# One matmul of 512 columns in place of two of 256 in the MLP's input product

## The chip, the cores and the metric

The kernel runs on one NeuronCore of a Trainium2 chip (trn2). The metric is the device time of one execution in microseconds, the median of three runs: 2261.78 us before the change (2261.63 to 2261.96).

## The reference

Two layers of a hybrid encoder over 256 tokens of width 2048, in float32. Each layer normalises x, projects it, runs two kinds of attention, projects back and adds; then comes the MLP that the change touches, with a hidden width of 8192:

```python
h = rmsnorm(x, mlp_norm[l])
u = jax.nn.relu(jnp.einsum('bsd,df->bsf', h, w_mlp_in[l]))
x = x + jnp.einsum('bsf,fd->bsd', u * u, w_mlp_out[l])
```

## The kernel before

**Precision.** TensorE multiplies in a reduced float32 format (fp32r). To keep the accuracy of float32, every operand is split into a high half (the value rounded to fp32r) and a low half (what is left), and a product is the sum of three: high by high, low by high, high by low.

**The weight stream.** All weights arrive as 384 slabs of 1 MB, [128, 2048], through SyncE's DMA queue into three `raw` buffers (`next_slab`, L112). Each slab is split in two pieces of 1024 columns: ScalarE writes the high half `whi` (L130), VectorE subtracts and writes the low half `wlo` (L131). There are four buffers of each, enough for two slabs.

**Two kinds of product.** `block_product` (L140) makes 256 tokens by 512 outputs: the activations are the stationary operand and 512 columns of a slab the moving one, so each of its matmuls moves 512 columns (L153 to L155), 24 of them per slab. `stationary_product` (L173) is turned round: 128 columns of the slab are stationary, and the moving operand is one half of the normalised, transposed activations, `h_t[k]`, 256 tokens wide. One slab holds all 16 blocks of 128 rows (k) for 128 outputs, and each k takes three matmuls: weight high by activation high (L180), weight high by activation low (L181), weight low by activation high (L182). `h_t[k]` is one tile [128, 2, 256], its two halves side by side.

**Who uses which.** The input and output projections and the MLP's second product go through `block_product`. The neighbourhood heads' q and k (32 slabs) and the MLP's first product (64 slabs in each of two layers, 128 in all) go through `stationary_product`.

**The MLP.** In four chunks (L519) of 16 slabs each, the first product leaves 128 hidden units by 256 tokens in a PSUM tile `accu`. ScalarE makes relu of it (`rl`, L524), VectorE multiplies the two (`u2`, L526), and `split` (L136, L137) makes the halves `u2T`, the stationary operand of the second product, which follows for the chunk's 16 slabs. PSUM accumulators (`acc`, `accu`) rotate through four buffers.

**What sets the order.** Weight loads keep the program's order. Everything else is ordered at build time by a scheduler that simulates the engines; each engine then executes its own list in that order. The scheduler mixes the end of one stage with the start of the next: at the start of an MLP the transposes of x (L221) stand between matmuls of the first slabs.

Of the kernel before, what the change touches and what calls it, by code (L numbers as in the profile page):

```python
# [18 lines left out]
P = 128  # L19
# [16 lines left out]
NB = 512  # L36
NEG = -1.0e30
RUN = 5 * RPB_C + GRID_W
# Where a query of column 0 and an even row finds its last neighbour in a head's reversed table.
RPB_FIRST = RPB_HEAD - 1 - (10 * RPB_C + GRID_W - 1 + WIN_C - 1)  # L40
N_CHUNK = 4
F_PER_CHUNK = D_FF // P // N_CHUNK
SLABS = 48 + 16 + 64 + 64
# Column blocks of 512 of the input projection: q, k, v of the differential heads 0-3, then 4-7.
DIFF_BLOCKS = [0, 2, 4, 1, 3, 5]
NA_Q, NA_K, NA_V = 3 * HALF, 4 * HALF, 5 * HALF

# [1 line left out]
def body(ctx, tc, x, x_t, w, gains_in, gains_o, final_g, lam_in, rpb, ident_in, rope_in, mask_in, out):  # L49
# [5 lines left out]
    small = ctx.enter_context(tc.tile_pool(name="small", bufs=4))  # L55
    ps = ctx.enter_context(tc.tile_pool(name="ps", bufs=2, space=PSUM))

# [1 line left out]
    gin = const.tile([P, 2 * DEPTH, NK], F32, name="gin")  # L59
    nc.scalar.dma_start(gin, gains_in)  # L60
    ident = const.tile([P, P], F32, name="ident")
# [3 lines left out]
    xs = [const.tile([P, D], F32, name=f"x{t}") for t in range(NT)]  # L65

    def stream(dst, src):
        """A load on the queue of the weights, in the order of the program."""
        tc.keep_in_program_order(nc.sync.dma_start(dst, src))

    lam_sb = [None]

    def load_table(l):
        """The relative position biases of a layer, from where each query reads its windows."""
        table = act.tile([P, HEADS, RUN + 1], F32, name="table", tag="table", bufs=1)
        for rr in range(P // GRID_W):
            src = bass.AP(tensor=rpb.tensor,
                          offset=rpb.offset + l * HEADS * RPB_HEAD + RPB_FIRST + rr * RPB_C,
                          ap=[[1, GRID_W], [RPB_HEAD, HEADS], [1, RUN]])
            stream(table[rr * GRID_W:(rr + 1) * GRID_W, :, :RUN], src)  # L80
        return table
# [23 lines left out]
    ones = const.tile([P, P], F32, name="ones")  # L105
    nc.vector.memset(ones, 1.0)

# [1 line left out]
    slab_no = [0]  # L109
    x_rest = [None]  # L110

# [26 lines left out]
                                       op0=ALU.mult, op1=ALU.subtract)  # L138

    def block_product(n_k, operand, before=None, split_tail=0):  # L140
        """[256, 512] = sum over n_k blocks of 128 of operand(k)^T @ the next slabs. The last
        `split_tail` slabs are held together, so that one tile of tokens ends before the other."""
        acc = [ps.tile([P, NB], F32, name="acc", tag="acc", bufs=4) for _ in range(NT)]
        parts = []
        todo = []

        def one(k, t):
            hi, lo = parts[k // 2]
            c0 = (k % 2) * NB
            a = operand(k)  # L150
            wh, wl = hi[:, c0:c0 + NB], lo[:, c0:c0 + NB]
            ah, al = a[:, 0, t * P:(t + 1) * P], a[:, 1, t * P:(t + 1) * P]
            nc.tensor.matmul(acc[t], ah, wh, start=k == 0, stop=False)  # L153
            nc.tensor.matmul(acc[t], al, wh, start=False, stop=False)  # L154
            nc.tensor.matmul(acc[t], ah, wl, start=False, stop=k == n_k - 1)  # L155

        n_s = n_k // 4
        for s in range(n_s):
            if before is not None:
                before(s)  # L160
            parts += next_slab()
            todo += range(4 * s, 4 * s + 4)
            if s < n_s - split_tail:
                for k in todo:
                    for t in range(NT):
                        one(k, t)
                todo = []
        for t in range(NT):
            for k in todo:
                one(k, t)  # L170
        return acc

    def stationary_product(h_t):  # L173
        """[128, 256] = the next slab^T @ normed activations, transposed."""
        parts = next_slab()
        acc = ps.tile([P, S], F32, name="accu", tag="acc", bufs=4)
        for k in range(NK):
            hi, lo = parts[k // 8]
            wh, wl = hi[:, (k % 8) * P:(k % 8 + 1) * P], lo[:, (k % 8) * P:(k % 8 + 1) * P]
            nc.tensor.matmul(acc, wh, h_t[k][:, 0], start=k == 0, stop=False)  # L180
            nc.tensor.matmul(acc, wh, h_t[k][:, 1], start=False, stop=False)  # L181
            nc.tensor.matmul(acc, wl, h_t[k][:, 0], start=False, stop=k == NK - 1)  # L182
        return acc

# [1 line left out]
    def rms_scale(ss, n, width):  # L186
        """(ss / width + EPS) ** -0.5 on [128, n]."""
        v = small.tile([P, n], F32, name="v")
        nc.gpsimd.tensor_scalar(v, ss, 1.0 / width, EPS, op0=ALU.mult, op1=ALU.add)
        r = small.tile([P, n], F32, name="r")  # L190
        nc.gpsimd.tensor_tensor(r, v, mhalf[:, :n], op=ALU.pow)
        return r

    class Norm:
        """RMSNorm of x in pieces: the gain goes into the transposed halves, the scale of
        each token comes out of `scale()` and is applied to the products."""

        def __init__(self, gain):
            self.gain = gain
# [12 lines left out]
            self.h_t[k] = h  # L212

        def take(self, n):
            """Columns n*512... of x are final."""
            for t in range(NT):
                self.squares(n, t)
            for k in range(4 * n, 4 * n + 4):
                pt = ps.tile([P, S], F32, name="tp", tag="tp", bufs=2)
                for t in range(NT):  # L220
                    nc.tensor.transpose(pt[:, t * P:(t + 1) * P], xs[t][:, k * P:(k + 1) * P], ident)  # L221
                self.store(k, pt)
# [5 lines left out]
                self._r[t] = rms_scale(tot, 1, D)  # L228
            return self._r[t]

# [1 line left out]
    def to_sbuf_rope(acc, r, which):  # L232
        """Rotary position of q (which 0) or k (which 1), then transposed: [(m d), head, token]."""
        dst = [act.tile([P, 4, S], F32R, name="qkT", tag="A", bufs=12) for _ in range(2)]
        for t in range(NT):
            nat = work.tile([P, NB], F32, name="nat", tag="nat", bufs=3)
# [41 lines left out]
        return hi, lo  # L278

    def along_free(r):  # L280
        """[128, 256]: r of every token, in all partitions."""
        pb = ps.tile([P, S], F32, name="tp", tag="tp", bufs=2)
        for t in range(NT):
            diag = work.tile([P, P], F32, name="diag", tag="o", bufs=4)
            nc.vector.tensor_scalar(diag, ident, r[t], None, op0=ALU.mult)
            nc.tensor.matmul(pb[:, t * P:(t + 1) * P], ones, diag, start=True, stop=True)
        rb = work.tile([P, S], F32, name="rb", tag="rb", bufs=1)
        nc.scalar.activation(rb, pb, AF.Copy)
        return rb

    def transposed_weights(pr):
        """[128 queries, tile, 256 keys] -> [128 keys, tile, 256 queries] in PSUM."""
        pw = ps.tile([P, NT, S], F32, name="tp", tag="tp", bufs=2)
        for t in range(NT):
            for kt in range(NT):
                nc.tensor.transpose(pw[:, kt, t * P:(t + 1) * P], pr[:, t, kt * P:(kt + 1) * P], ident)  # L296
        return pw

    def weights_times_v(pr, v, j):
        """pr [128 q, tile, 256 keys] -> [128 q, tile, 128] in PSUM."""  # L300
        pw = transposed_weights(pr)
        wt = work.tile([P, NT, S], F32, name="wT", tag="wT", bufs=3)
        nc.scalar.activation(wt, pw, AF.Copy)
# [5 lines left out]
        return po  # L309

    def to_mix(po, scale, gain):
        """Scaled rows of po, transposed, with the gain, split."""
        o = work.tile([P, NT, HD], F32, name="o", tag="o", bufs=4)
        for t in range(NT):
            nc.vector.tensor_scalar(o[:, t, :], po[:, t, :], scale[:, t:t + 1], None, op0=ALU.mult)
# [110 lines left out]
            else:  # L426
                nc.vector.scalar_tensor_tensor(sl, acc[t], scale[t], sl, op0=ALU.mult, op1=ALU.add)

# [1 line left out]
    norm = Norm(0)  # L430

    def prologue(s):
        """The transposed x comes in beside the first slabs, x itself and the tables behind them."""
        st = act.tile([P, 4, S], F32, name="xT", tag="A", bufs=12)

        def load(k0, k1):
            stream(st[:, k0:k1], x_t[s, :, k0:k1])
            for k in range(k0, k1):
                norm.store(4 * s + k, st[:, k, :])

        if s == 0:
            load(0, 2)
            x_rest[0] = lambda: load(2, 4)
        else:
            load(0, 4)

    for l in range(DEPTH):
        if l == 0:
            first = [block_product(NK, norm.h_t.__getitem__, before=b) for b in (prologue, load_constants)]
            for t in range(NT):  # L450
                for n in range(4):
                    norm.squares(n, t)
            # lambda, and the sub-norm's gain times 1 - lambda_init
            lq = lam_sb[0].rearrange("p l (a b) d -> p l a b d", b=2)
            prod = work.tile([P, DEPTH, 2, QKD], F32, name="prod", tag="o", bufs=4)
            for i in range(DEPTH):
# [62 lines left out]
        for c in range(N_CHUNK):  # L519
            us = []  # L520
            for f in range(F_PER_CHUNK):
                acc = stationary_product(h_t)
                rl = work.tile([P, S], F32, name="rl", tag="o", bufs=4)
                nc.scalar.activation(rl, acc, AF.Relu)  # L524
                u2 = work.tile([P, S], F32, name="u2", tag="o", bufs=4)
                nc.vector.tensor_mul(u2, acc, rl)  # L526
                if f % 2 == 0:
                    pair = act.tile([P, 2, 2, S], F32R, name="u2T", tag="A", bufs=12)
                split(pair[:, f % 2, 0], pair[:, f % 2, 1], u2, 1.0)
# [13 lines left out]
                        nxt.take(n)  # L543
        norm = nxt

# [1 line left out]
    for t in range(NT):  # L547
        r = norm.scale(t)
        for n in (3, 0, 1, 2):
# [27 lines left out]
def _pack_weights(w_in, w_out, w_mlp_in, w_mlp_out):  # L577
    slabs = np.empty((DEPTH, SLABS, P, 2048), np.float32)

    def moving(a):  # L580
        """[K, N] -> [N / 512, K / 512, 128, 4 * 512]"""
        K, N = a.shape
        a = a.reshape(K // NB, 4, P, N // NB, NB).transpose(3, 0, 2, 1, 4)
        return a.reshape(N // NB, K // NB, P, 2048)

    def stationary(a):
        """[2048, N] -> [N / 128, 128, 16 * 128]"""
        return a.reshape(NK, P, -1, P).transpose(2, 1, 0, 3).reshape(-1, P, 2048)

    for l in range(DEPTH):  # L590
# [54 lines left out]
```

## Time and profile before

| | |
|---|---|
| time, median of 3 | 2261.78 us |
| span of the profiled execution, first to last instruction | 2259.7 us |
| its own time | the span and what lies around it; 2.1 us separate the span from the median |
| TensorE matmul busy | 2244.5 us, 99%, 13904 matmuls |
| TensorE weight load busy | 2019.3 us, 89%, 13904 loads |
| VectorE, ScalarE, GpSimd busy | 57%, 47%, 4% |
| DMA | 183 GB/s mean over the span |
| mean granted TensorE clock | 0.999 of full speed |

How to read it: matmuls are pipelined, so one matmul's duration in the records (284 ns for 256 columns) is longer than the time it takes from the next one. What counts is the pitch: the distance from the start of one matmul to the start of the next. The chain that ended last gives each matmul its pitch, and the timeline gives starts.

### The profile page before, as it was taken

How to read it: one execution, taken by the hardware profiler on the slowest of the kernel's cores; microseconds unless marked ns; L12 is line 12 of the kernel's file. 1: busy time of each engine (PE TensorE's matmuls, PEld its weight loads, DVE VectorE, ACT ScalarE, POOL GpSimd, SP SyncE). 2: the span in 40 equal slices, each digit the busy share in tenths (PEclk: the TensorE clock that was granted, in tenths of full speed). 3: DMA queues.
4: the chain of work that ended last, by engine and by line, in shares of the span. 5: the costliest groups of instructions: out<-in, count | busy, mean ns of one | idle time of the engine just before them, and what ended most of it. 6: DMA issues, size and time to landing. Idle time of an engine off the chain costs nothing.

```text
span 2259.7 us, 33741 instructions
## 1 busy us (share of the span) xinstructions
PE 2244.5 (99%) x13904; PEld 2019.3 (89%) x13904; DVE 1296.5 (57%) x1615; ACT 1063.4 (47%) x1579; POOL 91.9 (4%) x136
## 2 busy tenths in 40 slices
PE   8999999999999999999999999999999999999998
PEld 7889998998998898899888899989989989988986
DVE  6656666655555555555566666665555555555554
ACT  6556454543444444344445564545434434444443
POOL 1111000000000000000010110000000000000000
PEclk9999999999999999999999999999999999999999
DMA  9453445555555545555654434455555555455553
GB/s 326 149 186 135 173 161 186 184 179 196 187 187 186 190 183 189 198 178 185 202 188 162 168 140 170 179 191 180 187 188 186 186 193 192 179 197 189 186 188 131
DMA packets 61306, 414.63 MB, mean 183 GB/s; under 512 B 7008, under 2 KB 9184, under 8 KB 11872
## 3 DMA queue, kind: packets, MB, share of 16 engines
q1 hardware_dynamic: 60720, 411.40, 50.8%
q8 instruction: 109, 1.79, 0.3%
q10 hardware_dynamic: 432, 1.08, 0.2%
q14 instruction: 45, 0.37, 0.0%
HBM read 410.35 MB, written 2.10 MB: 183 GB/s over the span
## 4 chain that ended last, share of the span: by engine, by line
PE 99%; DMA 0%; DVE 0%; ACT 0%; SPq 0%; issue 0%; POOL 0%; ACTq 0%; POOLq 0%
PE acc L155 18%; PE acc L153 18%; PE acc L154 18%; PE accu L180 14%; PE accu L182 14%; PE accu L181 14%; PE tp L307 1%; PE tp L296 1%; PE tp L221 0%; PE sc L343 0%; DMA raw<-in_w 0%; PE tp L257 0%; PE sc L345 0%; PE sc L344 0%; PE tp L412 0%; PE sc L387 0%
## 5 line engine op out<-in xcount | busy, mean ns | idle before, releaser
L131 DVE TENSOR_TENSOR wlo<-raw,whi 128x1024 fp32r<-128x1024 f32 (+1 forms) x770 | 945.7, 1229 | 848.0 <-ACT whi L130 841.4
L130 ACT ACTIVATE whi<-raw 128x1024 fp32r<-128x1024 f32 (+1 forms) x770 | 814.7, 1059 | 1055.5 <-PE acc L154 548.9
L181 PE MATMUL accu<-hT,whi 128*128 128x256 f32 x2560 | 726.0, 284 | 0.0
L182 PE MATMUL accu<-hT,wlo 128*128 128x256 f32 x2560 | 724.6, 283 | 0.0
L180 PE MATMUL accu<-hT,whi 128*128 128x256 f32 x2560 | 724.0, 283 | 0.0
L181 PEld LDWEIGHTS accu<-hT,whi 128*128 128x128 f32 x2560 | 491.5, 192 | 0.5
L180 PEld LDWEIGHTS accu<-hT,whi 128*128 128x128 f32 x2560 | 490.8, 192 | 0.8
L182 PEld LDWEIGHTS accu<-hT,wlo 128*128 128x128 f32 x2560 | 491.4, 192 | 0.0
L154 PE MATMUL acc<-whi,u2T 128*128 128x512 f32 x1024 | 399.2, 390 | 0.0
L153 PE MATMUL acc<-whi,u2T 128*128 128x512 f32 x1024 | 398.7, 389 | 0.0
L155 PE MATMUL acc<-wlo,u2T 128*128 128x512 f32 x1024 | 398.5, 389 | 0.0
L155 PEld LDWEIGHTS acc<-wlo,u2T 128*128 128x128 f32 x1024 | 192.3, 188 | 39.7
L153 PEld LDWEIGHTS acc<-whi,u2T 128*128 128x128 f32 x1024 | 192.3, 188 | 39.6
L154 PEld LDWEIGHTS acc<-whi,u2T 128*128 128x128 f32 x1024 | 192.3, 188 | 39.3
L153 PE MATMUL acc<-whi,hT 128*128 128x512 f32 x512 | 202.7, 396 | 6.0 <-ACT whi L130 6.0
L154 PE MATMUL acc<-whi,hT 128*128 128x512 f32 x512 | 203.0, 397 | 0.0
L155 PE MATMUL acc<-wlo,hT 128*128 128x512 f32 x512 | 199.4, 395 | 0.1
L153 PEld LDWEIGHTS acc<-whi,hT 128*128 128x128 f32 x512 | 96.9, 189 | 26.3 <-ACT whi L130 6.2
L155 PEld LDWEIGHTS acc<-wlo,hT 128*128 128x128 f32 x512 | 96.7, 189 | 20.3 <-DVE wlo L131 0.5
L154 PEld LDWEIGHTS acc<-whi,hT 128*128 128x128 f32 x512 | 96.9, 189 | 19.7
L154 PE MATMUL acc<-whi,mix 128*128 128x512 f32 x256 | 100.7, 393 | 0.0
L153 PE MATMUL acc<-whi,mix 128*128 128x512 f32 x256 | 100.7, 393 | 0.0
(117 smaller groups left out, 1331.9 us busy)
## 6 DMA issues: line engine op xcount, KB each, us to landing
raw<-in_w SPq DMA_DIRECT2D x383, 1024.0 KB, 4.8
x<-in_x SPq DMA_DIRECT2D x2, 1024.0 KB, 9.7
out<-xg SPq DMA_DIRECT2D x8, 256.0 KB, 3.1
table<-in_rpb SPq DMA_DIRECT2D x4, 438.0 KB, 11.5
xT<-in_x_t SPq DMA_DIRECT2D x3, 512.0 KB, 9.5
raw<-in_w SPq DMA_DIRECT2D x4, 256.0 KB, 5.4
gb<-in_final_g ACTq DMA_DIRECT2D x2, 512.0 KB, 5.7
xT<-in_x_t SPq DMA_DIRECT2D x2, 256.0 KB, 3.5
```

Source lines behind the costliest of these rows:

```text
L130: nc.scalar.activation(hi[:, c:c + step], r, AF.Copy)
L131: nc.vector.tensor_sub(lo[:, c:c + step], r, hi[:, c:c + step].bitcast(F32))
L153: nc.tensor.matmul(acc[t], ah, wh, start=k == 0, stop=False)
L154: nc.tensor.matmul(acc[t], al, wh, start=False, stop=False)
L155: nc.tensor.matmul(acc[t], ah, wl, start=False, stop=k == n_k - 1)
L180: nc.tensor.matmul(acc, wh, h_t[k][:, 0], start=k == 0, stop=False)
L181: nc.tensor.matmul(acc, wh, h_t[k][:, 1], start=False, stop=False)
L182: nc.tensor.matmul(acc, wl, h_t[k][:, 0], start=False, stop=k == NK - 1)
L296: nc.tensor.transpose(pw[:, kt, t * P:(t + 1) * P], pr[:, t, kt * P:(kt + 1) * P], ident)
L307: nc.tensor.matmul(po[:, t, :], wt[:, kt, t * P:(t + 1) * P], v[:, kt, j * HD:(j + 1) * HD], start=kt == 0, stop=kt == NT - 1)
```

## The change

`wide_product` takes the place of `stationary_product` in the MLP; the neighbourhood heads keep the old function. For each slab it first issues sixteen matmuls of the weights' high half against both activation halves at once (512 columns, `h_t[k]` flattened, into a PSUM tile `accw` of 512 columns), then sixteen of the weights' low half against the activations' high half (256 columns, added into the first 256 columns of `accw`). The columns 256 to 511 then hold the part low by high, and have to be added: ScalarE copies them to SBUF (`low`), VectorE adds the two parts (`whole`). VectorE makes relu and square in one operation on SBUF data, `max(u, 0) * u`. `low` is a new tile with two buffers, and the scratch space reserved for the DMA descriptors that GpSimd can write is set to 4096 bytes. Comments are gone, which shifts line numbers.

```diff
+    def wide_product(h_t):
+        parts = next_slab()
+        acc = ps.tile([P, NB], F32, name="accw", tag="acc", bufs=4)
+        for k in range(NK):
+            hi = parts[k // 8][0]
+            nc.tensor.matmul(acc, hi[:, (k % 8) * P:(k % 8 + 1) * P], h_t[k].rearrange("p a b -> p (a b)"),
+                             start=k == 0, stop=False)
+        for k in range(NK):
+            lo = parts[k // 8][1]
+            nc.tensor.matmul(acc[:, :S], lo[:, (k % 8) * P:(k % 8 + 1) * P], h_t[k][:, 0],
+                             start=False, stop=k == NK - 1)
+        low = work.tile([P, S], F32, name="low", tag="low", bufs=2)
+        nc.scalar.activation(low, acc[:, S:], AF.Copy)
+        whole = work.tile([P, S], F32, name="whole", tag="o", bufs=4)
+        nc.vector.tensor_add(whole, acc[:, :S], low)
+        return whole
...
             for f in range(F_PER_CHUNK):
-                acc = stationary_product(h_t)
-                rl = work.tile([P, S], F32, name="rl", tag="o", bufs=4)
-                nc.scalar.activation(rl, acc, AF.Relu)
+                u = wide_product(h_t)
                 u2 = work.tile([P, S], F32, name="u2", tag="o", bufs=4)
-                nc.vector.tensor_mul(u2, acc, rl)
+                nc.vector.scalar_tensor_tensor(u2, u, 0.0, u, op0=ALU.max, op1=ALU.mult)
...
-    nc = bacc.Bacc("TRN2", target_bir_lowering=False, num_devices=1)
+    nc = bacc.Bacc("TRN2", target_bir_lowering=False, num_devices=1, dynamic_dma_scratch_size=4096)
```

The next rows are TensorE's list before, in the middle of a chunk of the MLP's first product, where slab `whi_4315`/`wlo_4316` gives way to the next (`hT` numbers are the blocks k, 4026 the last, 3708 the first).

```order
L180 MATMUL accu_4319<-hT_4020,whi_4315 128x256
L181 MATMUL accu_4319<-hT_4020,whi_4315 128x256
L182 MATMUL accu_4319<-hT_4020,wlo_4316 128x256
L180 MATMUL accu_4319<-hT_4026,whi_4315 128x256
L181 MATMUL accu_4319<-hT_4026,whi_4315 128x256
L182 MATMUL accu_4319<-hT_4026,wlo_4316 128x256
L180 MATMUL accu_4385<-hT_3708,whi_4377 128x256
```

The same place now, first where a slab's high half ends and its low half begins.

```order
L192 MATMUL accw_4315<-hT_4014,whi_4311 128x512
L192 MATMUL accw_4315<-hT_4020,whi_4311 128x512
L192 MATMUL accw_4315<-hT_4026,whi_4311 128x512
L196 MATMUL accw_4315<-hT_3708,wlo_4308 128x256
L196 MATMUL accw_4315<-hT_3714,wlo_4308 128x256
L196 MATMUL accw_4315<-hT_3720,wlo_4308 128x256
```

Three matmuls of 256 columns per k became one of 512 and, sixteen matmuls later, one of 256; a slab's low half is first read in the second part of its slab.

VectorE's list before, over one slab of the same stage: the square, the activations' low half, and between them the two pieces of a later slab's low half.

```order
L526 TENSOR_TENSOR u2_4829<-accu_4778,rl_4827 128x256
L131 TENSOR_TENSOR wlo_4967<-raw_4964,whi_4966 128x1024
L137 SCALAR_TENSOR_TENSOR u2T_4765<-u2_4829,u2T_4765 128x256
L131 TENSOR_TENSOR wlo_4971<-raw_4964,whi_4970 128x1024
L526 TENSOR_TENSOR u2_4894<-accu_4843,rl_4892 128x256
```

VectorE's list now, over one slab (`accw_4572`, whose weights came as `raw_4562`; the slabs after it are 4614, 4665 and 4717).

```order
L201 TENSOR_TENSOR whole_4607<-accw_4572,low_4605 128x256
L543 SCALAR_TENSOR_TENSOR u2_4609<-whole_4607 128x256
L137 SCALAR_TENSOR_TENSOR u2T_4611<-u2_4609,u2T_4611 128x256
L131 TENSOR_TENSOR wlo_4720<-raw_4717,whi_4719 128x1024
L131 TENSOR_TENSOR wlo_4724<-raw_4717,whi_4723 128x1024
```

One operation per slab was added, the sum `whole`; the low half made behind it is that of the slab three further on.

At the start of an MLP, TensorE's list before, around the first use of a block (`hT_4008`) from the last 512 columns of x (`x0_79` and `x1_80` are x's two tiles, `tp` the transposes).

```order
L182 MATMUL accu_4123<-hT_3908,wlo_4120 128x256
L180 MATMUL accu_4057<-hT_4008,whi_4053 128x256
L180 MATMUL accu_4123<-hT_3914,whi_4119 128x256
L181 MATMUL accu_4123<-hT_3914,whi_4119 128x256
L182 MATMUL accu_4123<-hT_3914,wlo_4120 128x256
L180 MATMUL accu_4123<-hT_3920,whi_4119 128x256
L221 MATMUL tp_4017<-ident_75,x0_79 128x128
```

And now:

```order
L192 MATMUL accw_4160<-hT_3920,whi_4156 128x512
L192 MATMUL accw_4160<-hT_3926,whi_4156 128x512
L240 MATMUL tp_4017<-ident_75,x0_79 128x128
L240 MATMUL tp_4017<-ident_75,x1_80 128x128
L192 MATMUL accw_4057<-hT_4008,whi_4053 128x512
L192 MATMUL accw_4109<-hT_4008,whi_4105 128x512
L192 MATMUL accw_4160<-hT_4008,whi_4156 128x512
L240 MATMUL tp_4023<-ident_75,x0_79 128x128
```

Before, two slabs had been begun at that point; now three have, and 36 matmuls of 512 columns stand ahead of the first use of `hT_4008`. Outside the MLP's first product TensorE's and SyncE's lists hold the same instructions in the same order.

## Rows read from the trace of the kernel before

**Rows 1.** The page's first lines: span; busy time, share, instructions.

```profile
span 2259.7 us, 33741 instructions
PE 2244.5 (99%) x13904; PEld 2019.3 (89%) x13904; DVE 1296.5 (57%) x1615; ACT 1063.4 (47%) x1579; POOL 91.9 (4%) x136
```

**Rows 2.** The page's chain that ended last: shares by engine, by line.

```profile
PE 99%; DMA 0%; DVE 0%; ACT 0%; SPq 0%; issue 0%; POOL 0%; ACTq 0%; POOLq 0%
PE acc L155 18%; PE acc L153 18%; PE acc L154 18%; PE accu L180 14%; PE accu L182 14%; PE accu L181 14%; PE tp L307 1%; PE tp L296 1%; PE tp L221 0%; PE sc L343 0%; DMA raw<-in_w 0%; PE tp L257 0%; PE sc L345 0%; PE sc L344 0%; PE tp L412 0%; PE sc L387 0%
```

**Rows 3.** The waits of PE, whole run: total us, times, longest.

```profile
PE acc L153 <- ACT whi L130: 6.0, 1, 6.0
```

**Rows 4.** Timeline of PE, MLP first product: start us, us, instruction.

```profile
465.77 0.28 PE L181 MATMUL accu<-hT,whi 128*128 128x256 f32 x1
...
485.93 0.28 PE L181 MATMUL accu<-hT,whi 128*128 128x256 f32 x1
```

**Rows 5.** Timeline of PE, MLP second product.

```profile
509.69 0.39 PE L155 MATMUL acc<-wlo,u2T 128*128 128x512 f32 x1
...
549.81 0.39 PE L155 MATMUL acc<-wlo,u2T 128*128 128x512 f32 x1
```

**Rows 6.** Windows, first and second product: busy (x), PEclk, DMA share, GB/s.

```profile
430.00:490.00 60.00, 60.00 (x502) 60.00 (x501) 32.65 (x44) 28.16 (x42) 0.00 (x0) 1.00 0.54 190
510.00:570.00 60.00, 60.00 (x267) 49.69 (x266) 31.37 (x29) 23.34 (x22) 0.00 (x0) 1.00 0.54 193
```

**Rows 7.** Lines by form: count, busy us, mean ns, idle before, releasers.

```profile
L131 DVE TENSOR_TENSOR wlo<-raw,whi 128x1024 fp32r<-128x1024 f32 x766 | 942.9, 1232 | 846.1 <-ACT whi L130 839.5 <-PE tp L318 1.8 <-PE acc L154 0.2
L130 ACT ACTIVATE whi<-raw 128x1024 fp32r<-128x1024 f32 x766 | 812.2, 1061 | 1053.7 <-PE acc L154 548.9 <-PE accu L181 281.9 <-issue 206.4
L181 PE MATMUL accu<-hT,whi 128*128 128x256 f32 x2560 | 726.0, 284 | 0.0
...
L137 DVE SCALAR_TENSOR_TENSOR u2T<-u,u2T 128x256 fp32r<-128x256 f32 x128 | 53.6, 419 | 0.0
L526 DVE TENSOR_TENSOR u<-accu,rl 128x256 f32<-128x256 f32 x128 | 53.4, 417 | 0.0
L136 ACT ACTIVATE u2T<-u 128x256 fp32r<-128x256 f32 x128 | 51.2, 400 | 0.0
...
L524 ACT ACTIVATE rl<-accu 128x256 f32<-128x256 f32 x128 | 46.9, 367 | 0.0
...
L137 DVE SCALAR_TENSOR_TENSOR hT<-tp,gin,hT 128x256 fp32r<-128x256 f32 x48 | 21.5, 479 | 12.0 <-ACT hT L136 12.0
...
L136 ACT ACTIVATE hT<-tp,gin 128x256 fp32r<-128x256 f32 x48 | 20.7, 468 | 25.8 <-PE tp L221 25.8
```

**Rows 8.** The page's DMA issues: count, KB each, us to landing.

```profile
raw<-in_w SPq DMA_DIRECT2D x383, 1024.0 KB, 4.8
...
gb<-in_final_g ACTq DMA_DIRECT2D x2, 512.0 KB, 5.7
```

**Rows 9.** Timeline at the first MLP's start: PE, and VectorE's residual.

```profile
409.18 1.43 DVE L427 SCALAR_TENSOR_TENSOR x<-acc,r,x 128x512 f32<-128x512 f32 x2
...
409.65 0.28 PE L180 MATMUL accu<-hT,whi 128*128 128x256 f32 x1
...
415.34 0.40 PE L180 MATMUL accu<-hT,whi 128*128 128x256 f32 x2
```

## The prediction

> **What bounds the kernel now.** I read the chain that ended last first. TensorE holds 99% of it: three times 18% in the 512-column products and three times 14% in the 256-column ones [rows 2]. The table of waits agrees: in the whole run TensorE's matmuls wait once, 6.0 us at the start for the first slab [rows 3]. VectorE and ScalarE, at 57% and 47%, lie beside TensorE, which is busy 99% of the span [rows 1]. So the time is a count of matmuls times their pitch, and only a change of the count, of a pitch, or a new TensorE wait can show.
>
> The pitch has to come from starts, since matmuls overlap (284 ns in the records for one of 256 columns [rows 7]). In the MLP's first product, 168 steps lie between the starts at 465.77 and 485.93 us: 20.16 us / 168 = 120.0 ns per matmul of 256 columns [rows 4]. In the second product, 177 steps lie between 509.69 and 549.81: 40.12 / 177 = 226.7 ns per matmul of 512 columns [rows 5]. Two of 256 cost 240.0 ns, one of 512 costs 226.7. The difference over 256 columns, 106.7 ns, is 0.417 ns per column, one column per clock at the 2.4 GHz level that both stretches were granted (PEclk 1.00 [rows 6]); about 13.3 ns of each matmul do not depend on its columns. In both stretches TensorE is busy 60.00 of 60 us [rows 6], so no wait hides in either number.
>
> **The change part by part.**
>
> *Matmuls.* A slab took 48 of 256 columns: 48 x 120.0 = 5760 ns. It now takes 16 of 512 and 16 of 256. The latter are the same instruction as the third one before, with the same operands: 16 x 120.0 = 1920 ns. The former are new: weights stationary, 512 columns of activations moving. The trace has no such matmul. Its nearest row is the second product's, with the same columns, types and tile size and only the tensors exchanged: 226.7 ns. From above it is bounded by the two matmuls that it replaces, 240.0; from below by the columns alone, 512 x 0.417 = 213.4. I take 226.7: 16 x 226.7 = 3627 ns. The slab takes 3627 + 1920 = 5547 ns, 213 less. Over 128 slabs that is 27.3 us. With the bounds it is 0 us (240.0) and 54.5 us (213.4).
>
> A rule of the Trainium skill speaks against this size: "TensorE: Matmul & The Clock Gate", section "Back-to-back issue gap", gives a warm gap of the columns over 2.4 GHz and a fixed 2.5 ns. The rows put that fixed part at 13.3 ns in a stream where every matmul has a weight load of its own. By the page's figure, 2048 matmuls saved would give back 2048 x 2.5 ns = 5 us, an estimate from that page; the measured pitch decides.
>
> *Weight loads.* They fall with the matmuls, from 48 to 32 per slab. In the 256-column stretch they fill 60.00 of 60 us, in the 512-column stretch 49.69 [rows 6]. Whether the 120 ns are set by the columns or by the load, both pitches are measured with one load per matmul, as now. No term of its own.
>
> *Draining a slab.* Before: relu 367 ns on ScalarE and the square 417 on VectorE, then the split, 400 and 419. Now: the copy `low`, priced as the relu, 367; the sum `whole`, one PSUM and one SBUF input as the square had, 417; relu and square in one, SBUF to SBUF like the split's second half, 419; then the same split [rows 7]. Per slab VectorE goes from 2 x 1232 + 417 + 419 = 3300 ns to 3719, ScalarE stays at 2 x 1061 + 367 + 400 = 2889. Both are under the slab's 5547, so the 128 x 419 ns = 54 us added to VectorE lie beside the matmuls. If that cover were gone they would cost those 54 us.
>
> *The new wait.* `whole` waits for `low`, which ScalarE starts when the slab ends. Queued behind `whole` on VectorE stand relu-square, the split, and the two low pieces of the slab three further on, as the lists show. For the last slab of a chunk the second product is the reader, but of its last two blocks only (they share a tile), behind 14 others: at 6 matmuls each, 14 x 6 x 226.7 ns = 19 us. The drain is 367 + 417 + 419 + 400 + 419 = 2.0 us. For the others the waiting piece is a weight half: made when slab i+1 has ended, it is first read in the second part of slab i+3, a whole slab (5.5 us) and a high part (3.6 us) later, less the 2 x 1232 ns of making it. No cost. PSUM: `accw` takes a buffer of the same rotation of four, and drains some 2 us after its slab.
>
> *Weight buffers and the stream.* `whi` comes free sooner in its slab, `wlo` later: the first `wlo` piece after 3627 + 8 x 120 = 4587 ns, not after 2880. The new low half is needed no sooner than 3627 ns into its slab, so both ends move back together. The slab load lands in 4.8 us [rows 8]; a slab every 5.55 us asks less than the second product does, 24 x 226.7 = 5.44 us per slab at 193 GB/s with TensorE never waiting [rows 6]. No cost. The smaller descriptor space serves GpSimd, which issues no DMA (the page lists SP and ACT alone [rows 8]). Nothing.
>
> *An MLP's start.* Its last four activation blocks come out of the residual that ends at 409.18 + 1.43 = 410.61 us, 1.0 us into the MLP [rows 9]. Before, TensorE reached the first of them at 415.34, 5.7 us after 409.65 [rows 9]. Now 36 matmuls of 512 columns stand ahead of it, 36 x 226.7 = 8.2 us, so more cover. Then, however, only three matmuls lie between one block and the next, 0.68 us, and a block takes 468 + 479 = 947 ns to split [rows 7], if ScalarE and VectorE have nothing else. I take 0. From above: all four late by their whole split in both layers, 2 x 4 x 0.947 = 7.6 us. From below nothing: there is no TensorE wait here to win back [rows 3].
>
> **The sum.** Profiled execution: span 2259.7 - 27.3 = 2232.4 us. The median of the runs stands 2.1 us above that span, so 2232.4 + 2.1 = 2234.5 us, 1.2% faster.
>
> **The rivals.**
>
> *The pairing saves nothing.* The new matmul costs the bound, 240.0 ns, because fixed time hangs on the moving tile's halves and not on the instruction: 2261.8 us. Against it: 5376 matmuls of 512 columns are in this kernel and those of the long stretch take 226.7. For it: none of them moves `hT`.
>
> *Little fixed time per instruction.* If just a fifth of the 13.3 ns, 2.7, belonged to the instruction and the rest to what surrounds it, 2048 fewer would give 5.4 us: 2256.4. Against it: the two stretches share operand types and loads per matmul, and differ in the columns. The Trainium skill's section named above would make the fixed part about that small.
>
> *Slower: the drain becomes the bound.* Place: the ring of ScalarE and VectorE within a slab. If the two worked strictly in turn, each waiting for the other, a slab would take 2889 + 3719 = 6608 ns, 848 more than the 5760 of before: 128 x 0.848 = 108.5 us, 2370.3. It decides the sign as soon as the ring passes 5760. Against it: strictly in turn it would have been 2889 + 3300 = 6189 ns before, over 5760 already, yet TensorE never waited; within 60 us the two were busy 32.65 and 28.16 us [rows 6], and overlapped.
>
> **How the numbers follow.** Forecast 2234.5 with 0.90; no saving 2261.8 with 0.03; little fixed time 2256.4 with 0.03; the drain 2370 with 0.04. A measurement of this kernel tells 0.2%, 4.5 us, from no change. Faster: 0.90 + 0.03 = 0.93. Same: 0.03. Slower: 0.04. The range leaves the rivals out, since they hold 0.10: upwards it takes in the MLP starts' 7.6 us and about a microsecond of spread, to 2243; downwards a pitch 1.7 ns below 226.7 on 2048 matmuls, 3.5 us, to 2231. The bounds of 213.4 and 240.0 ns lie outside, each far from the nearest row.
>
> **What would show it.** In the profile after: 13904 - 2048 = 11856 matmuls; a pitch of 226.7 ns in the first part of a slab and 120.0 in the second; a slab every 5.55 us; TensorE's table of waits still near 6 us; VectorE about 54 us busier. The forecast is wrong if the 512-column pitch with `hT` moving is not 227, if TensorE waits for `wlo`, `accw` or `hT`, or if the granted clock is below 1.00 in the MLP.

## The result: 1.1% faster, some 3 us short of the forecast

The kernel before took 2261.72 us (2261.63 to 2261.96, 4 runs beside the new one), the changed kernel 2237.65 us (2237.55 to 2238.06, 4 runs): a ratio of 0.989, 95% interval 0.988 to 0.991. The forecast was 2234.5, with a range of 2231 to 2243. In the profiled execution of each, the span falls from 2259.7 to 2235.7 us, by 24.0, where the sum had 27.3.

The page's first lines after the change, and its chain that ended last, by engine and by line:

```profile
span 2235.7 us, 29767 instructions
PE 2220.2 (99%) x11856; PEld 1910.4 (85%) x11856; DVE 1349.1 (60%) x1743; ACT 1076.5 (48%) x1579; POOL 91.6 (4%) x136
...
PE 99%; DMA 1%; DVE 0%; ACT 0%; POOL 0%; issue 0%; ACTq 0%; POOLq 0%
PE accw L192 21%; PE acc L155 18%; PE acc L153 18%; PE acc L154 18%; PE accw L196 11%; PE accu L180 3%; PE accu L182 3%; PE accu L181 3%; PE tp L326 1%; PE tp L315 1%; PE tp L240 0%; DMA raw<-in_w 0%; PE sc L362 0%; PE tp L276 0%; PE sc L364 0%; PE sc L363 0%
```

Beside [rows 1] there are 2048 matmuls fewer, and 52.6 us more work on VectorE. Beside [rows 2] TensorE still holds 99% of the chain. The three lines of 14% each, 42 together, have become 21 + 11 for the new product and 9 for the attention's, which keeps the old one. TensorE's table of waits for the whole run (total us, times, longest) is as short as [rows 3]:

```profile
PE acc L153 <- ACT whi L130: 6.3, 2, 5.8
```

So no wait took the saving. It is in the pitch. Each MLP makes its first product in chunks of 16 slabs, and the start of a chunk and of the second product behind it are two rows of TensorE's timeline (start us, us, instruction). Before, first a chunk's first matmul, then the one after its last:

```profile
590.16 0.28 PE L180 MATMUL accu<-hT,whi 128*128 128x256 f32 x1
...
682.31 0.40 PE L153 MATMUL acc<-whi,u2T 128*128 128x512 f32 x1
```

After, the same chunk, with the groups of equal matmuls between:

```profile
587.80 3.79 PE L192 MATMUL accw<-hT,whi 128*128 128x512 f32 x16
591.42 2.08 PE L196 MATMUL accw<-hT,wlo 128*128 128x256 f32 x16
593.34 3.82 PE L192 MATMUL accw<-hT,whi 128*128 128x512 f32 x16
596.99 2.08 PE L196 MATMUL accw<-hT,wlo 128*128 128x256 f32 x16
598.90 1.32 PE L192 MATMUL accw<-hT,whi 128*128 128x512 f32 x5
...
676.84 0.40 PE L153 MATMUL acc<-whi,u2T 128*128 128x512 f32 x1
```

The chunk took 682.31 - 590.16 = 92.15 us and takes 676.84 - 587.80 = 89.04, or 5565 ns per slab. The sum had 5547. (Here and below, a count under a whole group means that the view's window ends inside the group.) The middle rows show where the 18 ns are. The first slab's wide matmuls, behind others of 512 columns, take 591.42 - 587.80 = 3.62 us, the sum's 16 x 226.7. The second slab's, behind narrow ones, take 596.99 - 593.34 = 3.65.

The starts of the single matmuls say more. In a slab behind narrow matmuls the first five wide ones take 233, 235, 228, 232 and 231 ns, and the others 226.7. The first two narrow ones behind wide ones take 113 and 119, then 120.0 each as in [rows 4]. Dearer and cheaper ones together make 18 ns per slab.

The whole account, chunk by chunk: the six chunks that are not an MLP's first each save 3.11 us, together 18.7. The first chunks of the two MLPs go from 93.44 to 90.52 and 90.49, and save 2.92 and 2.95. The first MLP starts 0.56 us later, at 410.21 instead of 409.65. The sum is 18.7 + 5.9 - 0.6 = 24.0 us, which is the difference of the spans. A chunk of the second product that has another chunk behind it takes 87.07 us in both, and the stage of the attention heads (from its first matmul of a q slab to the first of the output projection) 131.81.

The drain of a slab, in the lines grouped by form (count, busy us, mean ns of one, idle before):

```profile
L543 DVE SCALAR_TENSOR_TENSOR u<-whole 128x256 f32<-128x256 f32 x128 | 54.5, 426 | 4.2
L137 DVE SCALAR_TENSOR_TENSOR u2T<-u,u2T 128x256 fp32r<-128x256 f32 x128 | 54.4, 425 | 122.7 <-ACT u2T L136 122.7
L201 DVE TENSOR_TENSOR whole<-accw,low 128x256 f32<-128x256 f32 x128 | 53.6, 419 | 0.0
...
L199 ACT ACTIVATE low<-accw 128x256 f32<-128x256 f32 x128 | 49.0, 383 | 109.8 <-PE accw L196 109.8
```

These answer to [rows 7]: the prices of 419, 417 and 367 were 426, 419 and 383. A stretch of the first product, in the windows (busy us and count of PE, PEld, DVE, ACT and POOL, then the granted clock), shows that they lie beside the matmuls, TensorE being busy 56.00 of 56 us:

```profile
620.00:676.00 56.00, 56.00 (x326) 49.54 (x325) 35.48 (x50) 28.43 (x41) 0.00 (x0) 1.00 0.53 190
```

### The profile page after: what moved, and what is told of

Read it like the earlier page. It is cut to its first block, busy times and chain, and to the rows that moved or that the text cites. A ratio compares the mean times of both kernels' runs of the same rounds, so it can differ in the third digit from the quotient of the medians.

```text
span 2235.7 us, 29767 instructions
## 1 busy us (share of the span) xinstructions
PE 2220.2 (99%) x11856; PEld 1910.4 (85%) x11856; DVE 1349.1 (60%) x1743; ACT 1076.5 (48%) x1579; POOL 91.6 (4%) x136
## 4 chain that ended last, share of the span: by engine, by line
PE 99%; DMA 1%; DVE 0%; ACT 0%; POOL 0%; issue 0%; ACTq 0%; POOLq 0%
PE accw L192 21%; PE acc L155 18%; PE acc L153 18%; PE acc L154 18%; PE accw L196 11%; PE accu L180 3%; PE accu L182 3%; PE accu L181 3%; PE tp L326 1%; PE tp L315 1%; PE tp L240 0%; DMA raw<-in_w 0%; PE sc L362 0%; PE tp L276 0%; PE sc L364 0%; PE sc L363 0%
## 5 line engine op out<-in xcount | busy, mean ns | idle before, releaser
L131 DVE TENSOR_TENSOR wlo<-raw,whi 128x1024 fp32r<-128x1024 f32 (+1 forms) x770 | 934.7, 1228 | 632.3 <-ACT whi L130 504.7
L192 PE MATMUL accw<-hT,whi 128*128 128x512 f32 x2048 | 491.2, 391 | 0.0
L192 PEld LDWEIGHTS accw<-hT,whi 128*128 128x128 f32 x2048 | 376.1, 188 | 72.8
L196 PEld LDWEIGHTS accw<-hT,wlo 128*128 128x128 f32 x2048 | 262.8, 191 | 10.0
L196 PE MATMUL accw<-hT,wlo 128*128 128x256 f32 x2048 | 266.0, 283 | 0.0
L180 PE MATMUL accu<-hT,whi 128*128 128x256 f32 x512 | 145.6, 284 | 0.0
L181 PE MATMUL accu<-hT,whi 128*128 128x256 f32 x512 | 145.6, 284 | 0.0
L182 PE MATMUL accu<-hT,wlo 128*128 128x256 f32 x512 | 145.1, 283 | 0.0
L137 DVE SCALAR_TENSOR_TENSOR u2T<-u,u2T 128x256 fp32r<-128x256 f32 x128 | 54.4, 425 | 122.7 <-ACT u2T L136 122.7
```

Of the source, the lines that this page charges most:

```text
L131: nc.vector.tensor_sub(lo[:, c:c + step], r, hi[:, c:c + step].bitcast(F32))
L137: nc.vector.scalar_tensor_tensor(dst_lo, src, scale, dst_hi.bitcast(F32), op0=ALU.mult, op1=ALU.subtract)
L192: nc.tensor.matmul(acc, hi[:, (k % 8) * P:(k % 8 + 1) * P], h_t[k].rearrange("p a b -> p (a b)"), start=k == 0, stop=False)
L196: nc.tensor.matmul(acc[:, :S], lo[:, (k % 8) * P:(k % 8 + 1) * P], h_t[k][:, 0], start=False, stop=k == NK - 1)
```

## The experiments

The kernel before, run beside each, took between 2261.5 and 2261.8 us. The first four take the change apart, to find what the order is worth and where the 18 ns per slab come from. The next five look for versions that gain more, and for the cover of the drain. The last is a second try on the heads. In the edits shown, `<hi k>` and `<lo k>` stand for the 128 columns of block k in either half of the slab, and `...` for arguments left out.

**The order alone.** The new order with the old matmuls: high half first, two of 256 columns for each block, then the low half, and the old drain.

```
-            nc.tensor.matmul(acc, <hi k>, h_t[k].rearrange("p a b -> p (a b)"), ...)
+            nc.tensor.matmul(acc, <hi k>, h_t[k][:, 0], ...)
+            nc.tensor.matmul(acc, <hi k>, h_t[k][:, 1], ...)
```

> Leaves the widening out: 256-column matmuls with the old drain, but all products of a slab's high half first, then its low half. By the count-times-pitch theory nothing changes: 48 matmuls of 120.0 ns per slab, 5760 ns, about 2261.7 us, the kernel before. Rival, the order itself gave the gain (TensorE's list with the weights' two halves apart is quicker, or the weight buffers come free sooner): below 2255 us.

2261.77 us (10 runs), ratio 1.000 (0.999 to 1.001). The chunk in TensorE's timeline:

```profile
589.76 0.28 PE L191 MATMUL accw<-hT,whi 128*128 128x256 f32 x1
...
681.91 0.40 PE L153 MATMUL acc<-whi,u2T 128*128 128x512 f32 x1
```

That is 92.15 us, as before. With one width everywhere, the order is worth nothing, and the saving belongs to the wider matmuls. This kernel also keeps the descriptor space of 4096 bytes, so that is worth nothing either.

**Wide, but alternating.** The new matmuls, one wide and one narrow in turn, with the new drain.

```
         for k in range(NK):
             nc.tensor.matmul(acc, hi[:, c], h_t[k].rearrange("p a b -> p (a b)"), ...)
-        for k in range(NK):
             nc.tensor.matmul(acc[:, :S], lo[:, c], h_t[k][:, 0], ...)
```

> The widening alone: for each k the 512-column matmul and at once its 256-column one. The kernel after lost 26 ns on the first five wide matmuls behind a slab's narrow ones and won 8 back at the other passage, 18 ns net per slab (5565 ns where 5547 was forecast). Theory P, each passage from narrow to wide costs that: 16 passages, 5547 + 16 x 18 = 5840 ns per slab, 128 x 0.275 = 35 us over the kernel after, about 2273 us, slower than before. Theory R, only a run of narrow matmuls costs it, since the weight loads then lose their lead: 5547 ns, 2235.4 us. Theory D, it is the drain of the slab before (copy and sum reading PSUM): 5565 ns, 2237.6 us, with the dear matmuls where the drain lies.

2246.25 us, ratio 0.993 (0.992 to 0.995), between the numbers of all the theories. The chunk:

```profile
588.13 0.39 PE L193 MATMUL accw<-hT,whi 128*128 128x512 f32 x1
588.36 0.28 PE L194 MATMUL accw<-hT,wlo 128*128 128x256 f32 x1
588.47 0.40 PE L193 MATMUL accw<-hT,whi 128*128 128x512 f32 x1
...
678.57 0.40 PE L153 MATMUL acc<-whi,u2T 128*128 128x512 f32 x1
```

It takes 90.44 us, 5652 ns per slab or 353.3 per pair, where 226.7 + 120.0 make 346.7. A change of width and back costs 6.6 ns here, sixteen times in a slab, against 18 ns once in a slab of the changed kernel. So the cost neither goes away in alternation nor comes in full each time. Beside wide matmuls, "all sixteen first" is worth 2246.25 - 2237.65 = 8.6 us.

**The narrow matmuls of 384 columns.** The low half meets 384 of the 512 columns; the result holds one product too many, and its time alone is looked at.

```
-            nc.tensor.matmul(acc[:, :S], <lo k>, h_t[k][:, 0], ...)
+            nc.tensor.matmul(acc[:, :384], <lo k>, h_t[k].rearrange("p a b -> p (a b)")[:, :384], ...)
```

> The low half meets 384 columns, not 256 (adds half of the low by low products). Pitch by the line through 120.0 at 256 and 226.7 at 512: 173.3 ns. Theory R (the loads lose their lead only where a matmul is as short as a load): no passage cost, 16 x 226.7 + 16 x 173.3 = 6400 ns per slab, 128 x (6400 - 5565) = 106.9 us over the kernel after, 2344.5 us, and the first five wide matmuls of a slab at 226.7. Theory D (the drain): the first five at 233, 235, 228, 232, 231 as in the kernel after, 2346.9 us.

2352.20 us, ratio 1.040 (1.039 to 1.042). The chunk:

```profile
601.45 0.84 PE L192 MATMUL accw<-hT,whi 128*128 128x512 f32 x3
...
607.88 3.83 PE L192 MATMUL accw<-hT,whi 128*128 128x512 f32 x16
611.55 2.61 PE L196 MATMUL accw<-hT,wlo 128*128 128x384 f32 x14
...
704.88 0.39 PE L153 MATMUL acc<-whi,u2T 128*128 128x512 f32 x1
```

The narrow pitch settles at 173.3 ns, which is 13.3 + 384 x 0.417: the prediction's straight line through 120.0 and 226.7 holds at a third width. But a slab takes 103.43 / 16 = 6464 ns, 64 more than 16 x 226.7 + 16 x 173.3 = 6400. Behind 384 columns the first nine wide matmuls are dear (229, 233, 236, 224, 231, 236, 228, 232, 231), and the first six narrow ones are uneven (171 to 185). The theory by which the cost would vanish here is refuted; the other had its sign but not its size.

**All of 512 columns.** As the last, with 512 instead of 384.

> The low half meets both activation halves too (adds the low by low products): 32 matmuls of 512 columns per slab, all alike, the drain as before. Theories P and R: no passage, 32 x 226.7 = 7254 ns per slab, 216 us over the kernel after, 2454 us, every matmul of a slab at 226.7. Theory D: 26 ns more per slab, 2457 us, and the first five matmuls of a slab dear.

2453.13 us, ratio 1.085 (1.083 to 1.087). The chunk:

```profile
614.46 0.84 PE L192 MATMUL accw<-hT,whi 128*128 128x512 f32 x3
...
621.72 3.79 PE L192 MATMUL accw<-hT,whi 128*128 128x512 f32 x16
625.34 3.79 PE L196 MATMUL accw<-hT,wlo 128*128 128x512 f32 x16
628.97 1.30 PE L192 MATMUL accw<-hT,whi 128*128 128x512 f32 x5
...
730.51 0.39 PE L153 MATMUL acc<-whi,u2T 128*128 128x512 f32 x1
```

116.05 us are 512 matmuls of 226.7 ns: not one is dear (all starts lie 225 to 228 ns apart), though `low` and `whole` read the bank of a finished slab beside the next one's first matmuls as ever. So the cost does not come from the drain, nor from the change of accumulator. It needs a change of width.

**Two slabs at a time.** Both high halves first (32 wide), then both low halves (32 narrow), then both drains: half as many changes of width.

```
+        for acc, pt in zip(accs, parts):
+            for k in range(NK):   # high half of each of two slabs
+                nc.tensor.matmul(acc, <hi k>, h_t[k].rearrange("p a b -> p (a b)"), ...)
+        for acc, pt in zip(accs, parts):
+            for k in range(NK):   # then the low halves
+                nc.tensor.matmul(acc[:, :S], <lo k>, h_t[k][:, 0], ...)
```

> Two slabs together: 32 wide matmuls (16 of each), then 32 narrow ones, so half as many passages between the widths, everything else as in the kernel after, whose chunk of 16 slabs takes 89.04 us. Theory W (each passage there and back costs 18 ns, whatever the run's length): 16 x 5547 + 8 x 18 = 88.90 us per chunk, 128 x 9 ns = 1.2 us less in all, about 2236.5 us. Rival (the price grows with the narrow run before it): 89.04 us and no gain. If two drains at once or the weight buffers made TensorE wait, longer than 89.04.

2236.28 us (2236.09 to 2236.56), ratio 0.989 (0.987 to 0.990), 1.4 us below the changed kernel's 2237.65 and the fastest version of all. The chunk, and the waits of the whole run:

```profile
587.74 7.42 PE L191 MATMUL accw<-hT,whi 128*128 128x512 f32 x32
594.99 4.00 PE L197 MATMUL accw<-hT,wlo 128*128 128x256 f32 x32
598.82 7.44 PE L191 MATMUL accw<-hT,whi 128*128 128x512 f32 x32
606.10 4.00 PE L197 MATMUL accw<-hT,wlo 128*128 128x256 f32 x32
609.93 2.23 PE L191 MATMUL accw<-hT,whi 128*128 128x512 f32 x9
...
676.61 0.40 PE L153 MATMUL acc<-whi,u2T 128*128 128x512 f32 x1
```

```profile
PE acc L153 <- ACT whi L130: 6.3, 2, 5.9
```

88.88 us, where 88.90 was expected; above the 16 x 5547 = 88.75 of a chunk without any such cost stand 0.13 us, where the changed kernel has 0.29. The cost goes with the number of changes between long groups.

**The heads' products too.** The same wide product for the query and key slabs of the attention heads.

```
-        q = split_plain(stationary_product(h_t), [P, S], "half", 8)
-        acc = stationary_product(h_t)
+        q = split_plain(wide_product(h_t), [P, S], "half", 8)
+        acc = wide_product(h_t)
```

> The wide product for the neighbourhood heads' q and k as well, 32 more slabs. Count times pitch: 32 x (5760 - 5565) = 6.2 us less than the kernel after, 2231.4 us. Rival, the heads are bound by the way from q and k to the scores, which copy and sum make 0.8 us longer per head: gain under 2 us, or slower, with TensorE waits at the scores.

2258.3 us (2257.6 to 2260.6, 10 runs), ratio 0.999 (0.998 to 1.000): 20.7 us slower than the changed kernel, though 512 more matmuls were saved. The rival was right in its sign, for the heads' chain lost its cover; it was wrong in the place, since the heads' longest waits are not at the scores. The heads' stages grow from 131.81 to 140.09 and 139.78 us. One stretch of the first, in the windows of the changed kernel:

```profile
198.00:212.00 14.00, 14.00 (x120) 14.00 (x119) 9.95 (x17) 8.45 (x20) 2.03 (x4) 1.00 0.36 141
```

In the windows of this one, then some of its TensorE waits, then TensorE and VectorE in its timeline (in brackets the wait before, and what ended it):

```profile
198.00:212.00 14.00, 9.31 (x44) 7.46 (x43) 5.26 (x8) 5.54 (x13) 1.08 (x3) 0.76 0.30 110
```

```profile
PE tp L337 <- DVE o L334: 5.7, 2, 2.8
PE tp L429 <- ACT half L295: 2.7, 4, 0.7
PE tp L431 <- DVE half L296: 2.2, 4, 0.6
```

```profile
199.31 0.60 PE L315 MATMUL tp<-ident,wd 128*128 128x128 f32 x4
...
200.69 1.16 PE L326 MATMUL tp<-v,wT 128*128 128x128 f32 x8 [0.78 <-ACT wT L322]
...
204.28 0.61 DVE L334 TENSOR_SCALAR o<-tp,comb 128x128 f32<-128x128 f32 x2 [3.14 <-POOL comb L388]
204.68 0.73 PE L337 MATMUL tp<-ident,o 128*128 128x128 f32 x2 [2.84 <-DVE o L334]
...
207.34 2.50 PE L192 MATMUL accw<-hT,whi 128*128 128x512 f32 x5 [1.07 <-DVE vs L137]
```

L429 and L431 multiply a neighbourhood head's weights by its values. L315, L326 and L337 are steps of a differential head (transposing its weights, weights times values, transposing the output), and each needs what VectorE or ScalarE makes of the step before. The scheduler has now put these three close behind one another, without a slab's matmuls between, and TensorE waits 2.84 us for `o`, which waits for a scale from GpSimd.

Over the whole run TensorE's waits add up to 23.4 us, 17.1 more than in the changed kernel. The mean granted clock is 0.995 instead of 0.999, which over this span is an estimated 7 to 9 us. With the 6.2 us that the expectation saves taken off, the two make an estimated 18 to 20 us, and the spans differ by 2255.6 - 2235.7 = 19.9.

**More work on VectorE.** After `whole`, it is multiplied by 1.0 three, six or ten times: the values stay, only VectorE's work per slab grows.

```
         nc.vector.tensor_add(whole, acc[:, :S], low)
+        for _ in range(3):   # 6, 10
+            nc.vector.tensor_scalar(whole, whole, 1.0, None, op0=ALU.mult)
```

> Three more VectorE operations of 256 columns per slab (each multiplies the sum by 1), between the sum and relu-square. VectorE per slab: 3719 + 3 x 349 = 4766 ns of 5565. Theory that the drain lies beside the matmuls: 2237.7 us, no change from the kernel after. Rival, the drain's length is on the path: 128 x 3 x 0.349 = 134 us more.

> Six more: 3719 + 6 x 349 = 5813 ns of VectorE per slab, over the 5565 of the matmuls. Theory that the drain is hidden until VectorE's work per slab passes TensorE's: 128 x (5813 - 5565) = 32 us over the kernel after, less what the second product's stretches take up, 2250 to 2270 us. Rival, the ring with ScalarE binds sooner: above 2270.

> Ten more VectorE operations per slab, which took 292 ns each in the run with six: 2 x 1230 + 417 + 419 + 422 + 10 x 292 = 6638 ns of VectorE per slab, for the first time over the 5565 of the matmuls. Theory that the drain decides when VectorE's work per slab passes TensorE's: 128 x (6638 - 5565) = 137 us over the kernel after, about 2375 us, less some 10 us per chunk that the second product's stretch takes up: 2290 to 2375. Rival, something else would have to bind: no change, or well over 2375.

Three: 2237.44 us, ratio 0.990. Six: 2237.51, 0.989. Ten: 2332.82, 1.031 (1.030 to 1.033). With six, the windows, and the added line:

```profile
620.00:676.00 56.00, 56.00 (x325) 49.54 (x325) 50.65 (x112) 28.48 (x41) 0.00 (x0) 1.00 0.53 192
```

```profile
L203 DVE TENSOR_SCALAR whole<-whole 128x256 f32<-128x256 f32 x768 | 224.0, 292 | 18.2
```

An added operation takes 292 ns, not the 349 of the expectation. Six are 1.75 us per slab, an estimated 5.5 with the slab's own work, where the expectation had 5.8, over TensorE's 5.57. VectorE is at 50.65 of 56 us, and TensorE still waits for nothing. With ten, the windows, TensorE's longest waits, and two links of the chain that ended last (start us, us), behind which TensorE's next wide group starts at 667.95:

```profile
640.00:700.00 60.00, 51.47 (x284) 44.85 (x283) 50.85 (x120) 23.55 (x34) 0.00 (x0) 0.96 0.47 168
```

```profile
PE accw L192 <- ACT u2T L136: 55.2, 20, 2.8
PE acc L153 <- ACT whi L130: 7.1, 2, 5.7
```

```profile
667.04 0.44 DVE u L545
667.50 0.43 ACT u2T L136
```

At 292 ns each, ten are 2.9 us per slab more, and with the 3.7 of a slab's own VectorE work 6.6, above TensorE's 5.57. Now TensorE waits. VectorE itself is busy only 50.85 of the 60 us: the chain goes round from TensorE over VectorE and ScalarE and back, as in the prediction's rival. Of the 95.4 us by which this span (2331.1) exceeds the changed kernel's, waits behind the start are 61.8, and the mean granted clock, 0.986 for 0.999, is worth an estimated 30. The drain is a real bound, but 1.75 us more per slab on VectorE were still free.

**Pairs, and in the late heads.** Two slabs at a time, and also for query and key of heads 4 to 7 of the neighbourhood attention, away from the differential heads where the last try waited.

```
-        q = split_plain(stationary_product(h_t), [P, S], "half", 8)
+        qw, acc = wide_pair(h_t) if h >= 4 else (stationary_product(h_t), None)
+        q = split_plain(qw, [P, S], "half", 8)
```

> The paired order in the MLP, and paired wide products for q and k of the neighbourhood heads 4 to 7 alone, which have no differential head beside them. Theory that the widened heads lost by TensorE's waits beside the last differential heads: 16 slabs x 195 ns = 3.1 us less than the paired order alone, about 2233.2 us. Rival, the heads' own chain is short of matmuls to hide it, as the waits at its last products showed: slower than 2236.3.

2248.38 us, ratio 0.994 (0.993 to 0.996): 12.1 us slower than the pairs alone, and the rival was right: the heads' chain is short of cover away from the differential heads too. The heads' stages take 137.11 and 134.57 us. TensorE's waits:

```profile
PE accw L191 <- DVE whole L202: 5.4, 2, 3.2
PE tp L454 <- DVE half L317: 2.6, 2, 1.3
PE tp L452 <- ACT half L316: 1.4, 2, 0.7
```

## Why the prediction was right, step by step

- *The bound.* TensorE's count of matmuls times their pitch was the time, before and after. Right: the order alone moved nothing, and the four other orders and widths in the MLP moved the time by the pitches of their matmuls, with no more than 0.3 us of TensorE waits behind the start.
- *The wide matmul at 226.7 ns.* Right as a settled pitch with `hT` moving: behind wide ones the first part of a slab took 3.62 us, and 512 in a row took 116.05. The mis-sized term is "16 x 226.7 = 3627 ns" for wide ones behind narrow ones. Over a slab the passages add 18 ns, 2.3 us over 128 slabs. The prediction took its pitch from stretches of one width and did not price the change between them. The bound of 240.0 covered it.
- *The fixed part.* The Trainium skill ("TensorE: Matmul & The Clock Gate", section "Back-to-back issue gap") has 2.5 ns beside the columns, by which the gain would have been an estimated 5 us. It was 24, and three widths (120.0, 173.3 and 226.7 ns) lie on a line with 13.3 ns. The same section of the Trainium skill calls this the gap of an isolated matmul, and gives about 131 ns at 512 columns for a stream of pairs of weight load and matmul. The stream here is one of such pairs and took 226.7, so the trace bears out neither figure.
- *The drain and VectorE.* VectorE rose by 52.6 us, where 54 were forecast, and TensorE did not wait for it. The cover was larger than needed, as six added operations show. The rival was wrong here because the engines overlap: its ring shows in TensorE's waits only from somewhere between six and ten added operations.
- *The MLP's start, at 0.* The first chunks of the two MLPs saved 2.92 and 2.95 us, others 3.11, so about 0.2 us each was lost there, near the lower end of the 0 to 7.6.
- *The rest.* The 0.56 us before the first MLP were not forecast. They are there when the heads begin, at 185.25 instead of 184.69. In the other kernels that leave this part as it is, the MLP starts between 409.24 and 410.32 us, and once, with three added operations, at 411.99, so I take them for scatter.

Together 2.3 + 0.4 + 0.6 = 3.3 us: the sum's 27.3 against 24.0. What makes a passage dear stays open; every run that changed the moving width changed the width of the result with it. Shown is that it needs a change of width (all of 512), that it comes with each change between long groups (pairs), that it is smaller per change when widths alternate, and that it is larger between 512 and 384 columns than between 512 and 256. A weight load's record begins some 3 ns after the start of the matmul before, at either width, so the trace shows no lead that would be used up and built again; no theory that I formed gives all three sizes.

## What to carry to other kernels

Where TensorE is busy without a wait, count the matmuls and take each width's pitch from starts: one wide matmul for two narrow ones saves the fixed part, here 13.3 ns, and an equal width is best kept in long groups. Where TensorE's matmuls are the cover of another chain, as in the heads, the same edit takes cover away and can cost more than it saves. Work added to another engine is free only up to a point, which a few dummy operations find.

## What was not expected of the hardware

A change of the moving width costs time with no wait in the trace: 18 ns per slab between groups of sixteen at 512 and 256 columns, 64 ns at 512 and 384, and 6.6 ns per pair in alternation. And waits can cost more than themselves. Where TensorE was busy 9.31 of 14 us (the heads, 198 to 212 us), the granted clock was 0.76 on the mean, so part of that stretch ran at 1.2 GHz; the changed kernel, without waits there, had 1.00. The five wide matmuls behind the wait at 207.34 took 2.50 us, where five at the full clock took 1.32 (at 598.90 in the changed kernel). With ten added VectorE operations and 51.47 of 60 us busy it was 0.96.
